# Sums of h for both parts of the down product on GpSimd, and one ring for all its operands

## The chip, the cores and the metric

The kernel runs on one core of a Trainium2 chip, in one launch. The metric is the device time of the launch in microseconds (us). Times are given as the median of several runs; beside them stands one profiled execution with its trace.

## The reference

The reference is one inference step of a trunk of two layers. Layer 0 mixes along the sequence by retention, layer 1 by gated linear attention (GLA); after each mixer comes a feed-forward block with a short convolution. There are 1024 new rows of a prompt and 32 rows of a running stream, together T = 1056 rows; the model width is 1024, the inner width of the feed-forward block 2816. Everything is float32. The block that the change touches is this one:

```python
def conv_ffn(h, conv_state, w_up, conv_w, conv_b, w_down):
    u = h @ w_up                                     # 1024 -> 2 * 2816
    T = u.shape[1]
    ext = jnp.concatenate([conv_state.astype(u.dtype), u], axis=1)
    c = conv_b + ext[:, 0:T] * conv_w[0]
    for j in range(1, CONV_W):
        c = c + ext[:, j:j + T] * conv_w[j]
    gate, val = jnp.split(c, 2, axis=-1)
    return (jax.nn.silu(gate) * val) @ w_down, ext[:, T:]   # 2816 -> 1024
```

The trunk adds the block's result to its input. In what follows `h` is the product `silu(gate) * val`, and the last line's product with `w_down` is the down product.

## The kernel before, in words

**Tiles.** `h` is kept transposed, with its 2816 columns on 22 tiles of 128 partitions and the 1056 rows along each tile. The up product makes tile `f` of both halves (`gate`, `val`) in turn, f = 0 to 21, in `ffn_up`; the convolution of a tile (`conv`) follows a little later and stores the tile to `scr_h` in DRAM (L1563, L1564).

**Products.** Every float32 operand is split into a high and a low part, and a product of two operands is three matmuls (high × high L333, high × low L337, low × high L338). On top of that, blocks of two by two are multiplied by the scheme of Strassen and Winograd: seven products instead of eight, each of them (`seven`) 12 matmuls of 128x264. In return sums of the blocks are needed as operands: of the weights (`wg`, `ws`, `wt`, `wv`, made by VectorE from `rg` and `rv`; `wsh` and `wsl` are the high and the low part of `ws`), and of the activations.

**Down product.** The first 16 tiles of `h` go through this scheme in two parts of 8 tiles (p = 0, 1); the other 6 tiles are done by another routine. For each part there are four pairs q of output tiles and two token halves s; a unit is (p, q, s), and the order of units is p, then q, then s. For each part and token half seven operands are wanted, numbered 1, 2, 5, 6, 7, 4, 3: three of them plain blocks of `h`, four of them sums. An operand is split by ScalarE (cast, the high part) and VectorE (subtraction, the low part) into its place in `X[s]` (`XA`, `XB`). Part two's operands take the places of part one's, when the last unit of part one on that half is through.

**Part one's sums (before).** Four pairs of tiles, (0, 4) to (3, 7): both tiles of a pair are loaded (`load_h`, L1380) into a work space `v` in the large buffer `AR`, VectorE makes four sums in place (`sum_h`, L1386, 128x528 elements each) while the up product runs, at f = 9, 11, 13, 15, and the result is stored to `scr_s` in DRAM (`sums_out`, L1389). When the up product ends, `part_one` queues fourteen pieces of 528 KB, plain blocks from `scr_h` and sums from `scr_s`; they come through a ring of four slots in `AR` (`pull`, L1396), each split (L1411 cast, L1412 subtraction), and each split pulls the next piece.

**Part two's sums (before).** Two raw loads of 1.08 MB per token half (`staged`, L1418) bring the eight tiles, and VectorE makes the four sums (L1432, 128x1056) between the splits (L1427, L1428). For token half 0 the raw loads are issued at the start of unit (0, 1, 1), after all open splits are emptied; for half 1 at the end of unit (0, 3, 1).

**What sets the order.** Each engine runs its own instructions in a fixed order, and waits for semaphores. All DMAs here are issued by SP (SyncE), whose queue is in order too: an issue that waits holds up those behind it. In the code the order comes from lists of small closures (`todo`), of which `step` runs two after each product. A product index k = 7f + i counts products of the up product for token half 0; half 1 follows some products later. One period of f has 14 products. The vector engine's chain in a period is: the weights' sums (L310 to L316), the low parts (L306), the additions out of PSUM (L1532) and the convolution (L1558, L1559, L1562). GpSimd does only small copies and memsets there (L1545, L1547, L1555, L1556).

The functions that the change touches:

Of the kernel before, what the change touches and what calls it, by code (L numbers as in the profile page):

```python
# [9 lines left out]
F32 = mybir.dt.float32  # L10
# [6 lines left out]
P = 128  # L17
# [35 lines left out]
def trunk_kernel(ctx: ExitStack, tc: tile.TileContext, io):  # L53
# [1308 lines left out]

    class Pieces:


        def __init__(self, l, X, AR, sm, room, early):
            self.l, self.X, self.sm, self.room, self.early = l, X, sm, room, early
            self.stg = [AR[:, o:o + KT * TH].rearrange("p (k t) -> p k t", k=KT) for o in SX]
# [9 lines left out]
        def load_h(self, k, after):  # L1378
            for a in range(2):
                order(nc.sync.dma_start(self.v[:, a], scr_h[k + 4 * a].rearrange("p (q t) -> p q t", q=4)), after)  # L1380

        def sum_h(self, j):

            b11, b12, b21, b22 = [self.v[:, a, o::2] for a in range(2) for o in range(2)]
            d, a, b = [(b12, b12, b11), (b22, b22, b12), (b11, b22, b11), (b21, b22, b21)][j]
            V.tensor_tensor(d, a, b, op=ALU.subtract)  # L1386
# [12 lines left out]
        def part_one(self):  # L1399
            for s in range(2):  # L1400
                a, b = [slice(t, t + TH) for t in (CQ[2 * s][0], CQ[2 * s + 1][0])]
                lo, hi = scr_h[0:4], scr_h[4:8]
                sm_ = scr_s.rearrange("k p (a t) -> k p a t", a=2)
# [11 lines left out]

        def staged(self, p, s, j):
            c0 = CQ[2 * s + j][0]
            nc.sync.dma_start(self.stg[j], scr_h[KT * p:KT * p + KT, :, c0:c0 + TH].rearrange("k p t -> p k t"))  # L1418

        def operands(self, s):  # L1420
            X = self.X[s]
            lo, hi = slice(0, 4), slice(4, 8)
            b11, b21, b12, b22 = [x[:, k] for x in self.stg for k in (lo, hi)]

            def split(o, v):
                def run():
                    S.copy(X[o][:, 0], v)  # L1427
                    V.tensor_tensor(X[o][:, 1], v, X[o][:, 0].bitcast(F32), op=ALU.subtract)  # L1428
                return run

            def minus(d, a, b):
                return lambda: V.tensor_tensor(d, a, b, op=ALU.subtract)  # L1432

            self.todo += [split(1, b11), minus(b12, b12, b11), split(2, b21), split(5, b12), minus(b12, b22, b12),
                          split(6, b12), minus(b11, b12, b11), split(7, b11), minus(b21, b12, b21), split(4, b21),
                          split(3, b22)]
# [22 lines left out]
        def run(self):  # L1459
# [14 lines left out]
            def one(u, m):  # L1474
# [12 lines left out]
                if m == 3:  # L1487
# [3 lines left out]
                    if q == NPAIR - 1 and p == 0:  # L1491
                        while self.todo:
                            self.step()
                        if s:
                            for j in range(2):
                                self.staged(1, s, j)
                        self.operands(s)

            for n, u in enumerate(units):
                p, q, s = u  # L1500
                order_ = (1, 2, 5, 6, 7, 4) if q == 0 else (1, 2, 6, 5, 7, 4)
                for i, m in enumerate(order_):
# [4 lines left out]
                    if u == (0, 1, 1) and i == 0:  # L1507
                        while self.todo:
                            self.step()
                        for j in range(2):  # L1510
                            self.staged(1, 0, j)
# [3 lines left out]
                    self.step()  # L1515
# [3 lines left out]
    def ffn_up(l, X, todo, fc, sm, nxt, after):  # L1519
# [50 lines left out]
        for n, (_, s, k) in enumerate(sorted(seq)):  # L1570
# [3 lines left out]
            if f == NF - 1:  # L1574
                if s == 0 and i == 2:
                    nxt.part_one()
# [13 lines left out]
            if s == 1 and i % 2 == 0 and 8 <= f <= 16 and f % 2:  # L1590
                nxt.sum_h(i // 2)
            if s == 0 and i == 5 and 8 <= f <= 16:
                if f % 2 == 0:
                    if f > 8:
                        nxt.sums_out((f - 10) // 2)
                    if f < 16:
                        nxt.load_h((f - 8) // 2, stored[0])
# [240 lines left out]
def _layout(inp):  # L1838
# [10 lines left out]
    def cols(v):  # L1849
# [46 lines left out]
            "scr_w": (2, 2, NPAIR, 2, P, D), "scr_g": (16, P, T), "scr_s": (4, P, 2 * T), "scr_qk": (RH, 2, 2, P, T)}  # L1896
# [30 lines left out]
```

## Time and profile before

| | |
|---|---|
| median of 3 runs | 2854.89 us (2853.45 to 2854.96) |
| profiled execution | 2849.49 us, its span 2847.7 us |
| mean granted TensorE clock | 0.995 |
| busy: TensorE (PE) | 2784.6 us, 98% |
| busy: VectorE (DVE) | 2109.5 us, 74% |
| busy: ScalarE (ACT) | 1320.2 us, 46% |
| busy: GpSimd (POOL) | 278.5 us, 10% |

The profiled execution is one run of its own, and its time is a little under the three others. A row of the timeline gives the start in us from the span's start, the duration, the engine, the line in the kernel, the operation, and what it writes and reads; in brackets stands how long the engine had been idle and what ended that. A row of groups gives the count, the total busy time and the mean duration in ns. PE's busy time runs matmuls together that follow each other in the pipeline; where TensorE loses time is better read from the number of matmuls in a stretch.

In layer 0 the up product lies roughly at 915 to 1365 us of the span and the two parts of the down product follow until about 1545; in layer 1 the up product ends near 2585, and part two begins near 2680.

### The profile page before, as it was taken

Reading aid. Unit: us, or ns where it says so; the run is one execution under the profiler, and the core shown is the slowest. Engines: PE = TensorE matmul, PEld = TensorE weight load, DVE = VectorE, ACT = ScalarE, POOL = GpSimd, SP = SyncE. Lnnn points to the kernel's source line nnn. Section 1 sums busy time; section 2 is a strip of 40 time slices with the busy share of each in tenths; the row PEclk is TensorE's granted clock in tenths of the full one; section 3 lists DMA queues with packets and bytes.
Section 4 is the critical chain, followed back from the end, with each engine's and each line's share of the span. In section 5 each row is a group of like instructions: output and inputs, shape, how many; then the busy total and the mean of one; then the engine's idle time right before and its main releaser. Section 6 shows DMA issues by size and latency. Waiting matters only on the chain.

```text
span 2847.7 us, 52541 instructions
## 1 busy us (share of the span) xinstructions
PE 2784.6 (98%) x20954; PEld 2681.9 (94%) x20954; DVE 2109.5 (74%) x3506; ACT 1320.2 (46%) x2395; POOL 278.5 (10%) x516
## 2 busy tenths in 40 slices
PE   8999999999999999999999999999999999999998
PEld 7999977888999999999999899999999999999997
DVE  7777777777578877877775677774478878788756
ACT  8433344444455444445443555553245444445424
POOL 1000000000001111111000232220011111110001
PEclk9999999999999999999999999999999999999999
DMA  6333386664865223332866301114522233428673
GB/s 218 110 123 106 118 269 205 213 198 150 273 203 192 76 75 121 129 129 94 284 216 240 122 27 46 52 44 143 198 85 75 73 116 115 150 70 278 205 232 116
DMA packets 232326, 419.35 MB, mean 147 GB/s; under 512 B 27376, under 2 KB 145776, under 8 KB 231056
## 3 DMA queue, kind: packets, MB, share of 16 engines
q1 hardware_dynamic: 231536, 415.40, 43.6%
q8 instruction: 164, 2.69, 0.4%
q14 instruction: 82, 0.67, 0.1%
q10 hardware_dynamic: 544, 0.59, 0.1%
HBM read 292.08 MB, written 123.85 MB: 146 GB/s over the span
## 4 chain that ended last, share of the span: by engine, by line
PE 82%; DVE 7%; DMA 4%; ACT 4%; issue 1%; POOL 1%; SPq 0%; DVEq 0%; ACTq 0%; POOLq 0%
PE pu L338 16%; PE pu L333 16%; PE pu L337 16%; PE pd L1281 4%; PE pd L1280 4%; PE pd L1282 4%; PE psv L238 2%; PE psv L237 1%; PE psv L236 1%; PE pj L124 1%; PE pj L126 1%; PE pj L125 1%; PE pg L124 1%; PE pg L125 1%; PE pg L126 1%
## 5 line engine op out<-in xcount | busy, mean ns | idle before, releaser
L104 DVE TENSOR_TENSOR wlo<-raw,whi 128x1024 fp32r<-128x1024 f32 x146 | 180.7, 1241 | 100.9 <-ACT whi L104 44.9
L1536 ACT COPY AR<-pu 128x264 f32<-128x264 f32 x264 | 99.0, 375 | 295.2 <-PE pu L338 292.4
L338 PE MATMUL pu<-XA,wgl 128*128 128x264 f32 x752 | 213.6, 284 | 0.0
L333 PE MATMUL pu<-XA,wgh 128*128 128x264 f32 x752 | 213.0, 283 | 0.0
L337 PE MATMUL pu<-XA,wgh 128*128 128x264 f32 x752 | 213.0, 283 | 0.0
L104 ACT CAST whi<-raw 128x1024 fp32r<-128x1024 f32 x146 | 152.3, 1048 | 110.7 <-DMA raw<-w_ro 38.0
L1280 PE MATMUL pd<-XB,whi 128*128 128x264 f32 x552 | 157.9, 286 | 1.6 <-DVE rm L208 1.6
L1558 DVE SCALAR_TENSOR_TENSOR AR<-AR,cw 128x1058 f32<-128x1058 f32 x88 | 115.8, 1317 | 57.7 <-ACT AR L1557 57.4
L1282 PE MATMUL pd<-XB,wlo 128*128 128x264 f32 x552 | 157.0, 284 | 0.0
L1281 PE MATMUL pd<-XB,whi 128*128 128x264 f32 x552 | 156.7, 284 | 0.0
L333 PE MATMUL pu<-XA,wsh 128*128 128x264 f32 x520 | 148.6, 286 | 1.7 <-ACT AR L1536 0.9
L338 PE MATMUL pu<-XA,wsl 128*128 128x264 f32 x520 | 148.3, 285 | 0.8 <-DVE wsl L306 0.8
L337 PE MATMUL pu<-XA,wsh 128*128 128x264 f32 x520 | 147.7, 284 | 0.0
L1532 DVE TENSOR_TENSOR AR<-AR,pu 128x264 f32<-128x264 f32 (+2 forms) x440 | 144.6, 368 | 0.0
L306 DVE TENSOR_TENSOR wtl<-rv,wth 128x1024 fp32r<-128x1024 f32 x58 | 71.6, 1234 | 98.5 <-ACT wth L305 97.1
L333 PEld LDWEIGHTS pu<-XA,wgh 128*128 128x128 f32 x752 | 141.3, 188 | 0.0
L338 PEld LDWEIGHTS pu<-XA,wgl 128*128 128x128 f32 x752 | 141.2, 188 | 0.0
L337 PEld LDWEIGHTS pu<-XA,wgh 128*128 128x128 f32 x752 | 141.2, 188 | 0.0
L333 PE MATMUL pu<-XA,whi 128*128 128x264 f32 x448 | 127.5, 285 | 1.8 <-ACT XA L1427 1.2
L338 PE MATMUL pu<-XA,wlo 128*128 128x264 f32 x448 | 127.1, 285 | 1.6 <-DVE wlo L104 1.6
L337 PE MATMUL pu<-XA,whi 128*128 128x264 f32 x448 | 126.9, 284 | 0.5 <-DVE XA L1412 0.3
L333 PE MATMUL pu<-XA,wth 128*128 128x264 f32 x408 | 116.4, 285 | 0.7 <-ACT wth L305 0.7
(481 smaller groups left out, 10528.0 us busy)
## 6 DMA issues: line engine op xcount, KB each, us to landing
raw<-w_ro SPq DMA_DIRECT2D x52, 512.0 KB, 4.7
rg<-w_up SPq DMA_DIRECT2D x44, 512.0 KB, 3.6
rv<-w_up SPq DMA_DIRECT2D x44, 512.0 KB, 3.5
scr_h<-AR SPq DMA_DIRECT2D x44, 512.0 KB, 2.7
AR<-scr_x SPq DMA_DIRECT2D x32, 528.0 KB, 4.9
scr_x<-AR SPq DMA_DIRECT2D x32, 528.0 KB, 3.5
raw<-scr_w SPq DMA_DIRECT2D x32, 512.0 KB, 4.8
AR<-scr_h SPq DMA_DIRECT2D x28, 528.0 KB, 4.8
```

The source lines that it names most:

```text
L104: ins = S.copy(hi, raw), V.tensor_tensor(lo, raw, hi.bitcast(F32), op=ALU.subtract)
L124: PE.matmul(ps, hi[:, k], rh, start=kt == 0, stop=False)
L306: V.tensor_tensor(l_, src, h.bitcast(F32), op=ALU.subtract)
L333: mm = PE.matmul(ps, wh[:, k], x[:, 0, kt], start=m in (1, 2, 4, 5) and kt == 0, stop=False, skip_group_check=True)
L337: PE.matmul(ps, wh[:, k], x[:, 1, kt], start=False, stop=False, skip_group_check=True)
L338: mm = PE.matmul(ps, wl[:, k], x[:, 0, kt], start=False, stop=kt == 3, skip_group_check=True)
L1280: PE.matmul(o, w[0][:, k], h[0][:, :n], start=i == 0, stop=False)
L1281: PE.matmul(o, w[0][:, k], h[1][:, :n], start=False, stop=False)
L1282: self.last_mm = PE.matmul(o, w[1][:, k], h[0][:, :n], start=False, stop=i == nk - 1)
L1532: V.tensor_tensor(u[:, d:d + n], t[:, o:o + n], b[:, o:o + n], op=op)
L1536: S.copy(t, b)
L1558: V.scalar_tensor_tensor(cj, uj[:, 1:T + 3], cw[:, nt, 1:2], cj, op0=ALU.mult, op1=ALU.add)
```

## The change

All sums for both parts are now made ahead, by GpSimd. `sum_h` issues its subtraction on GpSimd in place of VectorE (line 1388 of the changed kernel). There are eight pairs of tiles instead of four, (0, 4) to (3, 7) and (8, 12) to (11, 15). A table `SUMS` says at which product k a pair is loaded; its four sums are called 5, 7, 9 and 11 products later, its store 12 later. `scr_s` in DRAM has eight entries instead of four.

`operands` queues 28 pieces instead of 14, both parts and both halves, and the pieces of part two come through the same ring of four slots (line 1398 of the changed kernel). The raw loads `staged`, the subtractions on VectorE for part two and the emptying of the list at unit (0, 1, 1) are gone. Between products one split is run instead of two, but for the units of q = 0 in part one.

```diff
+    SUMS = (42, 56, 70, 84, 97, 109, 121, 133)
...
-            self.stg = [AR[:, o:o + KT * TH].rearrange("p (k t) -> p k t", k=KT) for o in SX]
...
         def load_h(self, k, after):
             for a in range(2):
-                order(nc.sync.dma_start(self.v[:, a], scr_h[k + 4 * a].rearrange("p (q t) -> p q t", q=4)), after)
+                order(nc.sync.dma_start(self.v[:, a], scr_h[k + k // 4 * 4 + 4 * a].rearrange("p (q t) -> p q t", q=4)),
+                      after)
...
-            V.tensor_tensor(d, a, b, op=ALU.subtract)
+            G.tensor_tensor(d, a, b, op=ALU.subtract)
...
-        def part_one(self):
-            for s in range(2):
+        def operands(self):
+            for p, s in ((0, 0), (0, 1), (1, 0), (1, 1)):
                 a, b = [slice(t, t + TH) for t in (CQ[2 * s][0], CQ[2 * s + 1][0])]
-                lo, hi = scr_h[0:4], scr_h[4:8]
-                sm_ = scr_s.rearrange("k p (a t) -> k p a t", a=2)
+                lo, hi = scr_h[KT * p:KT * p + 4], scr_h[KT * p + 4:KT * p + 8]
+                sm_ = scr_s[4 * p:4 * p + 4].rearrange("k p (a t) -> k p a t", a=2)
...
-        def staged(self, p, s, j):
-            c0 = CQ[2 * s + j][0]
-            nc.sync.dma_start(self.stg[j], scr_h[KT * p:KT * p + KT, :, c0:c0 + TH].rearrange("k p t -> p k t"))
-
-        def operands(self, s):
...
-            self.todo += [split(1, b11), minus(b12, b12, b11), split(2, b21), split(5, b12), minus(b12, b22, b12),
-                          split(6, b12), minus(b11, b12, b11), split(7, b11), minus(b21, b12, b21), split(4, b21),
-                          split(3, b22)]
...
                         while self.todo:
                             self.step()
-                        if s:
-                            for j in range(2):
-                                self.staged(1, s, j)
-                        self.operands(s)
+                        self.splits()
...
-                    if u == (0, 1, 1) and i == 0:
-                        while self.todo:
-                            self.step()
-                        for j in range(2):
-                            self.staged(1, 0, j)
...
-                    self.step()
+                    self.step(1 if p or q else 2)
...
-                    nxt.part_one()
+                    nxt.operands()
...
-            if s == 1 and i % 2 == 0 and 8 <= f <= 16 and f % 2:
-                nxt.sum_h(i // 2)
-            if s == 0 and i == 5 and 8 <= f <= 16:
-                if f % 2 == 0:
-                    if f > 8:
-                        nxt.sums_out((f - 10) // 2)
-                    if f < 16:
-                        nxt.load_h((f - 8) // 2, stored[0])
+            for j, at in enumerate(SUMS if s == 0 else ()):
+                if k == at + 12:
+                    nxt.sums_out(j)
+                if k == at:
+                    nxt.load_h(j, stored[0])
+                if k - at in (5, 7, 9, 11):
+                    nxt.sum_h((k - at - 5) // 2)
...
-            "scr_w": (2, 2, NPAIR, 2, P, D), "scr_g": (16, P, T), "scr_s": (4, P, 2 * T), "scr_qk": (RH, 2, 2, P, T)}
+            "scr_w": (2, 2, NPAIR, 2, P, D), "scr_g": (16, P, T), "scr_s": (8, P, 2 * T), "scr_qk": (RH, 2, 2, P, T)}
```

GpSimd's order in the up product of layer 0. Before (the copies of the edges `cst` at L1555, L1556, the setting up of the next u buffer at L1545, L1547):

```order
L1547 COPY AR_7512<-cc_7507 128x2
L1545 MEMSET AR_7512 128x2x2
L1547 COPY AR_7512<-cc_7507 128x2
L1555 COPY cst_7508<-AR_7512 128x2
L1556 COPY cst_7508<-AR_7512 128x2
```

And of the changed kernel, where the same copies are lines 1527 and 1528 and the same setting up lines 1517 and 1519:

```order
L1517 MEMSET AR_7512 128x2x2
L1519 COPY AR_7512<-cc_7507 128x2
L1527 COPY cst_7508<-AR_7512 128x2
L1528 COPY cst_7508<-AR_7512 128x2
L1388 TENSOR_TENSOR AR_7512<-AR_7512 128x2x264 x4
L1527 COPY cst_7508<-AR_7512 128x2
L1528 COPY cst_7508<-AR_7512 128x2
```

The four sums of a pair stand directly one behind the other, between the edge copies of the two halves of one tile, although the code calls them two products apart.

SP's order in the same place of the changed kernel (1535 and 1536 store a tile of `h`, 1381 loads a pair, 299 and 300 load the weights `rg` and `rv`, 1391 stores the sums):

```order
L1535 DMA scr_h<-AR_7512 128x1024
L1536 DMA scr_h<-AR_7512 128x32
L1381 DMA AR_7512<-scr_h 128x1056 x2
L299 DMA rg_11500<-w_up 128x1024
L1391 DMA scr_s<-AR_7512 128x2112
L300 DMA rv_11501<-w_up 128x1024
```

The store of the sums, which waits for GpSimd, stands between the pair of weight loads of one f.

SP's order at the border from part one to part two, layer 0. Before (`scr_x` is the running result, loaded at L1480 and stored at L1489; 102 and 1444 load weights):

```order
L102 DMA raw_15949<-w_dn 128x1024
L1489 DMA scr_x<-AR_7512 256x1x528
L1480 DMA AR_7512<-scr_x 128x2x528
L102 DMA raw_15955<-scr_w 128x1024
L102 DMA raw_15961<-scr_w 128x1024
L1418 DMA AR_7512<-scr_h 128x8x264
L1489 DMA scr_x<-AR_7512 256x1x528
L1418 DMA AR_7512<-scr_h 128x8x264
L1444 DMA rv_15968<-w_dn 128x512
L1480 DMA AR_7512<-scr_x 128x2x528
```

And of the changed kernel (there 1460 and 1469 load and store the running result, 1424 loads weights):

```order
L1398 DMA AR_7512<-scr_s 128x4x264 x2
L102 DMA raw_15980<-w_dn 128x1024
L1469 DMA scr_x<-AR_7512 256x1x528
L102 DMA raw_15986<-scr_w 128x1024
L102 DMA raw_15992<-scr_w 128x1024
L1424 DMA rv_15999<-w_dn 128x512
L1398 DMA AR_7512<-scr_s 128x4x264
L1398 DMA AR_7512<-scr_h 128x4x264
```

The two raw loads are replaced by pieces, and the last two pieces of part two stand behind four weight loads.

More of the change, by code (lines that the diff above doesn't have):

```diff
@@ L1414, in splits @@
             self.todo += [run] * 7
-        def staged(self, p, s, j):
-            c0 = CQ[2 * s + j][0]
-            nc.sync.dma_start(self.stg[j], scr_h[KT * p:KT * p + KT, :, c0:c0 + TH].rearrange("k p t -> p k t"))
-        def operands(self, s):
[L1421 to L1432, printed above, removed]
-            self.todo += [split(1, b11), minus(b12, b12, b11), split(2, b21), split(5, b12), minus(b12, b22, b12),
-                          split(6, b12), minus(b11, b12, b11), split(7, b11), minus(b21, b12, b21), split(4, b21),
-                          split(3, b22)]
         def weights(self, p, q):
```

## The prediction

> **What bounds the kernel now.** I read the page's busy times first, then the windows of the two feed-forward layers, then the instructions around each place where TensorE loses time, and last the VectorE chain of the up product.
>
> ```profile
> PE 2784.6 (98%) x20954; PEld 2681.9 (94%) x20954; DVE 2109.5 (74%) x3506; ACT 1320.2 (46%) x2395; POOL 278.5 (10%) x516
> ```
>
> TensorE is busy for 98% of the span, and the change adds and removes no matmul. Its matmuls are modelled as pipelined, so the loss has to be read from their pace. These windows show it (columns: busy us and count of PE, PEld, DVE, ACT, POOL; granted clock; DMA share; GB/s):
>
> ```profile
> core 0: us, PE busy (x) PEld busy (x) DVE busy (x) ACT busy (x) POOL busy (x), PEclk, DMA share, GB/s
> 940.00:1340.00 400.00, 400.00 (x3299) 400.00 (x3298) 320.82 (x471) 183.12 (x258) 55.53 (x139) 1.00 0.30 104
> 1340.00:1395.00 55.00, 52.17 (x416) 50.69 (x415) 48.81 (x60) 34.78 (x44) 3.37 (x8) 1.00 0.84 274
> 1450.00:1490.00 40.00, 37.64 (x286) 36.45 (x285) 30.45 (x37) 16.26 (x23) 0.00 (x0) 0.96 0.65 217
> 2560.00:2620.00 60.00, 57.63 (x460) 56.17 (x459) 52.38 (x65) 36.66 (x47) 3.60 (x10) 1.00 0.78 256
> 2675.00:2715.00 40.00, 37.29 (x296) 36.18 (x295) 31.52 (x37) 16.97 (x25) 0.00 (x0) 1.00 0.68 226
> ```
>
> In the up product of layer 0 (940 to 1340) TensorE never waits: 400.00 / 3299 = 0.12125 us per matmul, which is the pace of this kernel. Against it, 1450 to 1490 loses 40.00 − 286 × 0.12125 = 5.3 us, and 2675 to 2715 loses 40.00 − 296 × 0.12125 = 4.1 us. These two are the borders from part one to part two of the down product, 9.4 us together. The granted clock is 0.96 in the first of them; the windows without a wait have 1.00, so I count that to the wait, and if it has a cause of its own, 0.04 × 40 = 1.6 us of the 5.3 stay. The other two, 55.00 − 416 × 0.12125 = 4.6 and 60.00 − 460 × 0.12125 = 4.2 us, are the way from the up product into the down product; there the ring of four slots runs already, and the change leaves its first pieces as they are.
>
> What is late at the border of layer 0 (start, duration, engine, line; the bracket is idle time and what ended it):
>
> ```profile
> 1458.00 0.28 PE L338 MATMUL pu<-XA,wv 128*128 128x264 f32 x1
> 1459.29 0.39 PE L333 MATMUL pu<-XA,whi 128*128 128x264 f32 x1 [1.02 <-ACT XA L1427]
> 1460.27 0.39 PE L333 MATMUL pu<-XB,whi 128*128 128x264 f32 x1 [0.59 <-ACT XB L1427]
> 1467.05 0.39 PE L333 MATMUL pu<-XB,whi 128*128 128x264 f32 x1 [0.55 <-ACT XB L1427]
> 1458.17 1.07 ACT L1427 CAST XA<-AR 128x1056 fp32r<-128x1056 f32 x1 [2.64 <-DMA AR<-scr_h]
> 1450.17 0.38 SPq L1418 DMA_DIRECT2D AR<-scr_h  x1
> 1454.95 0.56 SPq L1489 DMA_DIRECT2D scr_x<-AR  x1
> 1455.56 0.72 SPq L1418 DMA_DIRECT2D AR<-scr_h  x1
> ```
>
> The chain runs from the raw loads of token half 1 (L1418): the second is issued only at 1455.56, behind a store of results (L1489). ScalarE waits 2.64 us for the first, TensorE waits for ScalarE's cast, and the subtractions (L1432) stand between the later casts. Only four loads per layer do this, but TensorE needs all seven operands of the half within one unit.
>
> **The change, part by part.** *Part two's raw loads and subtractions go.* These are the costs that leave (DVE rows: count | busy us, mean ns):
>
> ```profile
> L1432 DVE TENSOR_TENSOR AR<-AR 128x1056 f32<-128x1056 f32 x16 | 20.0, 1253 | 4.6 <-DMA AR<-scr_h 4.6
> L1386 DVE TENSOR_TENSOR AR<-AR 128x528 f32<-128x528 f32 x32 | 22.5, 705 | 6.2 <-DMA AR<-scr_h 6.1
> L1428 DVE TENSOR_TENSOR XA<-AR,XA 128x1056 fp32r<-128x1056 f32 x16 | 19.9, 1253 | 11.9 <-ACT XA L1427 7.9 <-PE pu L338 3.8
> DMA to landing us min/median/max: 6.3/7.3/8.1
> DMA to landing us min/median/max: 3.9/5.0/6.2
> DMA to landing us min/median/max: 3.9/4.7/5.7
> ```
>
> VectorE is rid of 20.0 us in the down product and 22.5 us in the up product. Neither is time by itself: VectorE is off the path except at the borders. What counts is that the wait is gone with its cause: 5.3 + 4.1 = **−9.4 us**, if the new feed keeps up. The three last rows are the landing times of the raw loads (L1418), of the ring's pieces (L1396) and of the pair loads (L1380); a piece lands in 5.0 us where a raw load took 7.3.
>
> *Part two's operands come by the ring.* One slot's cycle is load, cast and subtraction: 5.0 + 1.07 + 1.25 = 7.3 us, so four slots give one piece per 1.83 us. A product takes 12 × 0.12125 = 1.455 us and uses one piece, so the ring is slower than TensorE and lives on its lead: the units of part one's last pairs need no new pieces. I walked the fourteen pieces of part two through SP's and VectorE's new order, with landing times as above. Pieces 8 to 12 (token half 1) are ready between 1446.9 and 1456.7, before TensorE wants the first at 1458.1. The 13th and 14th pull stand on SP behind four weight loads of the next pair; they are ready at 1465.7 and 1466.9, wanted at 1458.1 + 5 × 1.455 = 1465.4 and some four products later. So the thirteenth is about 0.3 us late, by a walk that is itself good to about a microsecond. Bounds: nothing from below, from above what the same ring loses at its first use, 4.6 + 4.2 = 8.8 us. I take 1.0 us per layer, **+2.0 us**, near the lower end: at its first use the ring starts with two pieces and an empty lead, here with four and a lead of two units.
>
> *All 32 sums per layer go to GpSimd, in the up product.* In the new order the four sums of a pair stand directly behind each other, so GpSimd works in 8 bursts per layer, 16 in all, every second f. The trace has no such instruction of 128x528 elements; nearest are (POOL rows):
>
> ```profile
> L943 POOL TENSOR_TENSOR d<-b 128x384 f32<-128x384 f32 x56 | 51.0, 918 | 137.5 <-DVE x L951 57.1 <-DVE b L925 40.6 <-DVE gss L1133 39.5
> L149 POOL TENSOR_TENSOR ss<-ss,sq 128x264 f32<-128x264 f32 x24 | 22.6, 941 | 294.8 <-ACT sq L138 292.9 <-DVE XB L1254 1.9
> ```
>
> GpSimd has room (55.53 of 400 us). The question is what VectorE loses meanwhile. At the program's start both do the same kind of sum at once:
>
> ```profile
> 13.03 5.06 POOL L149 TENSOR_TENSOR NB<-NB 128x384 f32<-128x384 f32 x3 [12.59 <-ACT NB L138]
> 13.42 1.84 DVE L149 TENSOR_TENSOR NB<-NB 128x384 f32<-128x384 f32 x2
> 15.18 2.03 DVE L104 TENSOR_TENSOR wlo<-raw,whi 128x1024 fp32r<-128x1024 f32 x1
> 17.14 1.36 DVE L149 TENSOR_TENSOR NB<-NB 128x384 f32<-128x384 f32 x1
> 30.28 0.55 DVE L149 TENSOR_TENSOR NB<-NB 128x384 f32<-128x384 f32 x1
> 9.10 1.23 DVE L104 TENSOR_TENSOR wlo<-raw,whi 128x1024 fp32r<-128x1024 f32 x1 [1.12 <-ACT whi L104]
> ```
>
> Alone VectorE's four would take 3 × 0.55 + 1.23 = 2.88 us; beside GpSimd they take 13.42 to 18.50, 5.08 us. So three GpSimd sums cost VectorE 2.2 us, 0.73 each, or 0.73 × 528/384 = 1.0 each of the new ones: 4.0 us per burst. GpSimd's own burst is then 4 × 5.06/3 × 528/384 = 9.3 us. Bounds for VectorE's loss: 0 if the two do not meet, and the dearest row, 941 ns for 264 elements, taken whole: 4 × 2 × 0.94 = 7.5 us.
>
> The Trainium skill, page "SBUF — State Buffer", in its section on the two separate sides of the memory, says that VectorE and GpSimd share a pair of ports under an exclusive lock held for a whole instruction, which a VectorE instruction with two operands in SBUF takes part in. The trace agrees in kind (2.03 against 1.23 us); by that rule alone every GpSimd sum would stand in VectorE's way in full, which is the upper bound's case and the second rival below.
>
> Who waits for VectorE is the weights. Its chain in one period of the up product:
>
> ```profile
> 1170.64 1.22 DVE L306 TENSOR_TENSOR wsl<-rg,wsh 128x1024 fp32r<-128x1024 f32 x1
> 1171.89 0.33 SPq L300 DMA_DIRECT2D rv<-w_up  x1
> 1175.55 0.69 DVE L310 TENSOR_TENSOR rv<-rv 128x512 f32<-128x512 f32 x1
> 1178.81 1.23 DVE L306 TENSOR_TENSOR wtl<-rv,wth 128x1024 fp32r<-128x1024 f32 x1 [2.57 <-ACT wth L305]
> 1183.67 0.29 PE L338 MATMUL pu<-XA,wtl 128*128 128x264 f32 x1
> 1176.44 1.22 SPq L1380 DMA_DIRECT2D AR<-scr_h  x2
> ```
>
> A period is fourteen products of 1.455 us, 20.4 us. `wsl` frees the buffer for the next load, that load feeds L310, and `wtl` stands behind L310. A delay of `wsl` is taken up by the 2.57 us in which VectorE waits for ScalarE and by the 1183.67 − 1180.04 = 3.63 us until TensorE uses `wtl`: 6.2 us of cover. A burst begins when the pair has landed (1176.44 + 4.7, plus the issue of two), some nine microseconds ahead of the next `wsl`, so its 4.0 us reach `wsl` nearly whole. 4.0 < 6.2: **0 us**. Without cover left it would be 7.5 − 6.2 = 1.3 us per burst, 16 × 1.3 = 21 us. Between bursts lie two periods, in which VectorE has 20% idle (320.82 of 400), some 8 us: the delay is worked off.
>
> *Added waits.* The store of the sums (L1391 of the change) waits on SP for GpSimd, and behind it stands the next weight load `rv`. That load waits for `wsl` anyway, and the burst (1182 to 1191) ends ahead of the delayed `wsl` of the next period (1170.64 + 20.4 + 1.2 + 4.0 = 1196): nothing, and a burst that lasted 5 us longer would make the store the later one. Behind the burst on GpSimd stand the small copies and memsets of the two u buffers, wanted a period later: nothing. Part two's stored sums add 4 × 1.08 MB per layer against removed raw loads, in windows where the DMA queues are 0.30 busy: nothing.
>
> **Sum:** −9.4 + 2.0 + 0 = −7.4 us. Against the profiled execution, 2849.5 us (span 2847.7 and 1.8 around it), that gives 2842.1. The median of the runs is 2854.9, 5.4 above, so I forecast **2847.5 us** on the median. Between 2845.5 (no ring loss) and 2849 lies the forecast's own range.
>
> **Rivals.** *The ring is as slow as at its first use.* For it: the cycle of 1.83 us against 1.455, and the pulls that stand behind weight loads. Against it: four slots are filled early. Then 8.8 of the 9.4 us come back, −0.6: 2854 us, no change.
>
> *GpSimd keeps VectorE out for longer than the cover.* One mechanism at one place: `wtl` comes late in every f with a burst. For it, with VectorE only 20% idle, stands a two-column copy on GpSimd that took 1.22 us while VectorE was at work, and 0.19 us after:
>
> ```profile
> 1167.83 1.31 DVE L1559 SCALAR_TENSOR_TENSOR AR<-AR,cw 128x1058 f32<-128x1058 f32 x1
> 1167.98 1.22 POOL L1556 COPY cst<-AR 128x2 f32<-128x2 f32 x1
> 1169.28 0.19 POOL L1547 COPY AR<-cc 128x2 f32<-128x2 f32 x1
> ```
>
> So they exclude each other at least in part. Against it: 0.73 us per sum of 384 measured, and VectorE's additions out of PSUM need not meet it. It decides from 6.2 us per burst; at 7.5 us the time is 2847.5 + 21 = 2868 us, slower.
>
> *The sums come too late.* The last pair is loaded at k = 133 of 154 and its sums are stored by 145, while the ring first wants a sum of part two after the whole of part one; I give this nothing of its own.
>
> **Chances.** Forecast 0.58, ring as slow as before 0.24, GpSimd in the way 0.18. A measurement of this kernel tells about 0.2% (5.7 us) from no change; the forecast lies 7.4 below, so its chance is that of faster, 0.58; same 0.24, slower 0.18. The range runs from 2843.5 (the whole 9.4 and 2 more for VectorE's relief) to 2859, which holds the first rival and the mild end of the second, where the cover is passed by a quarter of a microsecond per burst.
>
> **What would show it.** Right: the borders' windows at 0.12125 us per matmul with at most 1 us lost each, no wait for XB above a few tenths; L1388 on GpSimd at 1.3 to 2.3 us each; TensorE without a wait in 940 to 1340, `wtl` done ahead of its matmul though L306 and L1530 show stretched instances. Wrong: waits of `pu<-XA,wtl` or of `wsl` on VectorE in every second f (the second rival); waits on ring pieces behind weight loads at the borders (the first); or a border's loss that stays although the operands are early, which would mean that the weights or the results were late there too.

## The result and the profile after

The changed kernel takes 2870.01 us (median of 5 runs, 2864.05 to 2876.39); the kernel before, timed beside it, 2853.45 us (5 runs, 2852.31 to 2854.96). The ratio is 1.0057, with a 95% interval of 1.0038 to 1.0077: some 16 us **slower**, where 2847.5 us and faster was forecast and 2859 was the upper end of the range. The profiled execution took 2864.05 us, span 2862.2 us, 14.5 us more than before.

The busy times of the changed kernel, and the same stretches of its span as shown of before (busy us and count of PE, PEld, DVE, ACT, POOL; granted clock; DMA share; GB/s):

```profile
PE 2783.5 (97%) x20954; PEld 2678.2 (94%) x20954; DVE 2121.3 (74%) x3458; ACT 1318.6 (46%) x2395; POOL 398.2 (14%) x580
940.00:1340.00 400.00, 394.28 (x3219) 392.46 (x3218) 327.70 (x446) 178.58 (x252) 108.22 (x167) 1.00 0.36 124
1450.00:1490.00 40.00, 39.08 (x317) 38.41 (x316) 30.16 (x37) 20.57 (x29) 0.00 (x0) 1.00 0.90 308
2165.00:2560.00 395.00, 387.80 (x3174) 385.70 (x3174) 326.01 (x441) 177.15 (x250) 109.05 (x165) 1.00 0.35 123
2675.00:2715.00 40.00, 37.89 (x307) 37.25 (x307) 32.80 (x39) 21.89 (x31) 0.00 (x0) 1.00 0.94 312
```

At 0.12125 us per matmul the up product of layer 0, which lost nothing before, now loses 400.00 − 3219 × 0.12125 = 9.7 us, that of layer 1 395.00 − 3174 × 0.12125 = 10.2. VectorE is busy for 7 us more in layer 0's (327.70 against 320.82), although it makes 16 sums fewer. The border of layer 0 loses 1.6 us where it lost 5.3.

The kernels do not reach the same work at the same time, so a second reading is used from here on: the start of the n-th matmul in one trace minus the start of the n-th in the other, over the same n. It gives what a stretch costs (us; stretches named by the times of the kernel before, minus is a gain):

| kernel | up product, layer 0 (940 to 1340) | border, layer 0 (1395 to 1490) | up product, layer 1 (2165 to 2560) | border, layer 1 (2600 to 2715) |
|---|---|---|---|---|
| changed kernel | +9.4 | −3.7 | +7.9 | 0.0 |

Which wait it is shows in the groups of TensorE. First the row of before, then that of the changed kernel (the first of three matmuls with the weights `wsh`; count, busy us, mean ns, idle before and what ended it):

```profile
L333 PE MATMUL pu<-XA,wsh 128*128 128x264 f32 x520 | 148.6, 286 | 1.7 <-ACT AR L1536 0.9 <-DVE AR L1532 0.7
```

```profile
L333 PE MATMUL pu<-XA,wsh 128*128 128x264 f32 x520 | 150.1, 289 | 14.7 <-DVE AR L1504 12.6 <-ACT AR L1508 1.6
```

Not the weights are late, but L1504, VectorE's addition out of PSUM. Of the eight bursts per layer seven end in such a wait, of 0.15 to 1.84 us, always at product m = 3 of token half 0. The longest in layer 0, with VectorE's work ahead of it, GpSimd's burst, and TensorE's wait (changed kernel):

```profile
1271.87 1.22 DVE L306 TENSOR_TENSOR wgl<-rg,wgh 128x1024 fp32r<-128x1024 f32 x1
1273.01 1.81 DVE L315 TENSOR_TENSOR wv<-rv,wv 128x512 fp32r<-128x512 f32 x1
1274.75 1.81 DVE L311 TENSOR_TENSOR rg<-rv,rg 128x512 f32<-128x512 f32 x1
1276.48 0.38 DVE L1504 TENSOR_TENSOR AR<-AR,pu 128x232 f32<-128x232 f32 x1
1276.79 1.51 DVE L312 TENSOR_TENSOR rg<-rg 128x512 f32<-128x512 f32 x1
1278.22 1.82 DVE L316 TENSOR_TENSOR rv<-rv,rg 128x512 f32<-128x512 f32 x1
1280.06 1.31 DVE L1531 SCALAR_TENSOR_TENSOR AR<-AR,cw 128x1058 f32<-128x1058 f32 x1
1281.29 0.42 DVE L1504 TENSOR_TENSOR AR<-AR,pu 128x264 f32<-128x264 f32 x1
1272.52 6.97 POOL L1388 TENSOR_TENSOR AR<-AR 128x528 f32<-128x528 f32 x4 [3.92 <-DMA AR<-scr_h]
1281.76 0.39 PE L333 MATMUL pu<-XA,wsh 128*128 128x264 f32 x1 [1.84 <-DVE AR L1504]
```

The same place in the kernel before, a few periods earlier:

```profile
1184.27 1.22 DVE L306 TENSOR_TENSOR wgl<-rg,wgh 128x1024 fp32r<-128x1024 f32 x1
1185.41 0.68 DVE L315 TENSOR_TENSOR wv<-rv,wv 128x512 fp32r<-128x512 f32 x1
1186.01 0.68 DVE L311 TENSOR_TENSOR rg<-rv,rg 128x512 f32<-128x512 f32 x1
1186.62 0.39 DVE L1532 TENSOR_TENSOR AR<-AR,pu 128x232 f32<-128x232 f32 x1
1186.92 0.68 DVE L312 TENSOR_TENSOR rg<-rg 128x512 f32<-128x512 f32 x1
1187.52 0.68 DVE L316 TENSOR_TENSOR rv<-rv,rg 128x512 f32<-128x512 f32 x1
1189.46 0.42 DVE L1532 TENSOR_TENSOR AR<-AR,pu 128x264 f32<-128x264 f32 x1
1192.16 0.28 PE L333 MATMUL pu<-XA,wsh 128*128 128x264 f32 x1
```

Before, `wgl` starts at 1184.27 and the addition ends at 1189.88: 5.61 us; then 2.28 us pass until TensorE starts m = 3. In the changed kernel the same way takes 1271.87 to 1281.71, 9.84 us: 4.23 us more. 4.23 − 2.28 = 1.95 us, and TensorE starts m = 3 2.0 us late. The code says why m = 3 waits there: it adds into the PSUM bank `c` which m = 5 filled, and the addition for m = 7 must have read that bank before. So this is a wait inside the scheme of seven products; by the code another PSUM bank would not lift it, which no run tried.

The stretching itself is one for one. Four VectorE instructions with both operands in SBUF (`wv`, L311, L312, L316, each 0.68 us before, as their rows show) are 1.13, 1.13, 0.83 and 1.14 us longer, one for each sum; the addition with an operand in PSUM that lies among them is not (0.38 us, 0.39 before). More such additions fall beside sums in a later run, the kernel with the burst behind m = 3: there 58 of them (128x264) take 0.42 us in the median, like the 191 others in the two up products. The Trainium skill, page "SBUF — State Buffer", section "Who interferes with whom", says that VectorE with two SBUF inputs and a GpSimd instruction that reads SBUF block each other for a whole instruction, and that VectorE with at most one SBUF input does not take part unless it runs in a mode that uses two ports; these rows agree with both halves of it.

### The profile page after: what moved, and what is told of

The parts are those of the page before. It is cut to its first block, busy times and chain, and to the rows that moved or that the text cites. A ratio compares the mean times of both kernels' runs of the same rounds, so it can differ in the third digit from the quotient of the medians.

```text
span 2862.2 us, 52654 instructions
## 1 busy us (share of the span) xinstructions
PE 2783.5 (97%) x20954; PEld 2678.2 (94%) x20954; DVE 2121.3 (74%) x3458; ACT 1318.6 (46%) x2395; POOL 398.2 (14%) x580
## 2 busy tenths in 40 slices
DMA packets 242247, 443.15 MB, mean 155 GB/s; under 512 B 28080, under 2 KB 152624, under 8 KB 239952
## 4 chain that ended last, share of the span: by engine, by line
PE 73%; DVE 13%; DMA 5%; ACT 4%; issue 3%; POOL 1%; SPq 0%; DVEq 0%; ACTq 0%; POOLq 0%
PE pu L333 14%; PE pu L338 14%; PE pu L337 13%; PE pd L1281 3%; PE pd L1280 3%; PE pd L1282 3%; PE psv L238 2%; PE psv L237 2%; PE psv L236 2%; DVE wgl L306 1%; PE pj L124 1%; PE pj L126 1%; PE pj L125 1%; PE pg L124 1%; PE pg L125 1%
## 5 line engine op out<-in xcount | busy, mean ns | idle before, releaser
L1504 DVE TENSOR_TENSOR AR<-AR,pu 128x264 f32<-128x264 f32 (+2 forms) x440 | 144.1, 366 | 0.0
L149 POOL TENSOR_TENSOR ss<-ss,sq 128x264 f32<-128x264 f32 (+2 forms) x39 | 38.9, 997 | 745.7 <-ACT sq L138 743.8
L1529 ACT ACTIVATE AR<-AR,cw 128x1058 f32<-128x1058 f32 x88 | 111.9, 1271 | 55.8 <-DVE AR L1504 52.6
L333 PE MATMUL pu<-XA,whi 128*128 128x264 f32 x448 | 127.3, 284 | 2.0 <-ACT AR L1451 1.9
```

The lines of the kernel that those rows point to most:

```text
L333: mm = PE.matmul(ps, wh[:, k], x[:, 0, kt], start=m in (1, 2, 4, 5) and kt == 0, stop=False, skip_group_check=True)
L1504: V.tensor_tensor(u[:, d:d + n], t[:, o:o + n], b[:, o:o + n], op=op)
L1529: S.activation(cj, uj[:, 2:T + 4], AF.Identity, scale=cw[:, nt, 2:3], bias=cw[:, nt, 3:4])
```

## The experiments

**One chip, four kernels: who makes the sums, how many, how they are spaced, and where.** The theory is that VectorE's 4.2 us are passed on to TensorE where an addition has only 2.3 us of cover. The rivals are the doubled pair loads and stores, GpSimd's own queue, and a cost for every sum without a threshold. The kernel before had 2849.64 us there; chips differ by a few us, so each ratio is against the kernel before on the same chip.

All sums on VectorE:

```diff
-            G.tensor_tensor(d, a, b, op=ALU.subtract)
+            V.tensor_tensor(d, a, b, op=ALU.subtract)
```

> The changed kernel with one edit: the 32 sums per layer are made by VectorE instead of GpSimd; pairs, stores and the ring are as in the change. Theory: four GpSimd sums in a row lengthen VectorE's instructions beside them by about 4.2 us, one addition out of PSUM behind them then frees its PSUM bank too late (it has 2.3 us of cover), and TensorE waits in 7 of 8 bursts per layer; that is the 9.7 and 10.2 us lost in the two up products. On VectorE a sum takes 0.7 us and the four do not stand together in its order, so TensorE should not wait in 940 to 1340 and 2165 to 2560: about 20 us less than the changed kernel, 2846 to 2851 us. Rival one, the doubled pair loads and stores on SP and the DMA queues: nothing changes, 2865 to 2870. Rival two, GpSimd's edge copies and memsets stand behind the sums and the u buffers come late: also 2846 to 2851, so this run does not part it from the theory.

Measured 2849.33 us, ratio 0.9994 (0.9985 to 1.0003). The up product at pace:

```profile
940.00:1340.00 400.00, 400.00 (x3297) 399.85 (x3296) 332.09 (x490) 183.72 (x257) 58.52 (x140) 1.00 0.36 125
```

The doubled loads and stores are all there (DMA share 0.36, as in the changed kernel) and cost the up product nothing. That rival falls. VectorE is busier than in the changed kernel (332.09 against 327.70 us) and still in time.

Two of four sums:

```diff
-                if k - at in (5, 7, 9, 11):
+                if k - at in (5, 7):
```

> The changed kernel with two of the four sums of each pair left out (the other two are stored unsummed, so the result of the down product is not the reference's). A burst is half as long. Theory (a cover of 2.3 us, then a wait): half a burst costs VectorE about 2.1 us, so hardly any wait of TensorE for an addition is left, 0 to 0.3 us per burst; 2846 to 2852 us. Rival, every GpSimd sum costs TensorE its share, without a threshold: half of the 20 us stays, about 2860 us. Rival, transfers: 2865 to 2870.

Measured 2848.31 us, ratio 0.9993 (0.9984 to 1.0002). Half a burst costs the up products nothing at all, not half. So where these bursts fall there is a threshold, and it lies between two and four sums in a row.

Each sum paced by the product beside which it is called:

```diff
-            G.tensor_tensor(d, a, b, op=ALU.subtract)
+            tc.add_manual_dep(G.tensor_tensor(d, a, b, op=ALU.subtract).ins, mm.ins.name,
+                              mybir.DependencyInfo(mybir.DependencyClass.Sync, mybir.DependencyReason.DATA),
+                              reason="pace")
```

> The changed kernel with one edit: each sum on GpSimd also waits for the last matmul of the product beside which it is called, so the four of a pair start some 5.8 us apart (two products of each token half) instead of one behind the other. Theory: each sum costs VectorE about 1 us, less than the 2.3 us of cover, and VectorE has a fifth of its time to make it up before the next: no wait of TensorE in the up products; 2846 to 2851 us, below the kernel before. Rival, GpSimd's own queue (edge copies and memsets behind the sums): the queue is now blocked for over 20 us per pair instead of 7, so it gets worse than 2870. Rival, transfers: nothing changes, 2865 to 2870.

Measured 2853.74 us, ratio 1.0011 (1.0001 to 1.0020): the 16 us are gone, as the theory had it, but the time was above the 2846 to 2851 expected, though the profiled execution (2849.27 us) loses nothing between 940 and 1340 and between 2165 and 2560 us. A second series of the same kernel, at the end of the study, asked whether pacing has a cost of its own.

> The kernel whose GpSimd sums are each paced by a product, once more: its runs had a median 4 us over the kernel before although its profiled execution showed no wait in the up products. If that was one chip's spread, it now stands within 2 us of the kernel before; if pacing has a cost of its own (GpSimd's edge copies and memsets behind a waiting sum), it stands 3 to 6 us above it again, and the profile of this execution should show TensorE waiting in the up products or at the borders.

It gave 2851.52 us against 2850.67, ratio 1.0002 (0.9992 to 1.0011). By the medians most of the 4 us were spread between series. The traces show a cost all the same, just behind the stretches above: by the n-th matmul both paced executions lose 2.5 and 2.2 us between 1340 and 1395 and 1.5 and 1.2 us between 2560 and 2600, where the kernel with the burst behind m = 3 loses nothing. There the first two pieces of the ring stand on SP behind the store of the last sums; in the first paced execution they are issued at 1333.64, against 1328.11 with the burst behind m = 3, and TensorE waits twice for the addition (0.22 and 0.70 us). That the late ring is the reason is likely, but not shown. Within the up products the rival falls: GpSimd's queue, in which the four sums of a pair now stretch over 19 us, costs nothing there.

Part one's sums alone on GpSimd, in the kernel before:

```diff
             d, a, b = [(b12, b12, b11), (b22, b22, b12), (b11, b22, b11), (b21, b22, b21)][j]
-            V.tensor_tensor(d, a, b, op=ALU.subtract)
+            G.tensor_tensor(d, a, b, op=ALU.subtract)
```

> The kernel before with one edit: part one's 16 sums per layer are made by GpSimd; part two is as before, with raw loads and VectorE's subtractions, and there are no more loads or stores than before. Theory: four bursts per layer, each a wait of about 1.2 us with what follows, some 8 to 10 us more than the kernel before, 2861 to 2864 us; the borders to part two lose their 5.3 and 4.1 us as before. Rival, transfers: the time of the kernel before, 2853 us.

Measured 2856.7 us, ratio 1.0023 (1.0013 to 1.0033): slower by 6.6 us, without a single added transfer. Two of its four bursts per layer end in a wait for the addition, of 0.64 to 0.93 us, and a third in layer 0 in one of 0.12 us. 8 to 10 us were expected: the sign and the place are the theory's, the size is not, since not every burst meets the addition. That asked for the next runs.

**Same burst, other place.** If the place in VectorE's period decides, then four sums in a row must be free at one place and dear at another. On one chip (the kernel before 2849.78 us) ran the changed kernel once more, and two in which the burst waits for a chosen product of token half 0:

> The changed kernel as it is, once more, so that it stands on one chip beside the next three. Theory and rivals alike: 12 to 20 us over the kernel before, with waits of TensorE at product m = 3 (pu<-XA,wsh) in 7 of 8 bursts per layer.

2868.48 us, ratio 1.0064 (1.0050 to 1.0078), with waits at m = 3 behind all eight bursts of layer 0 and six of layer 1.

Burst behind product m = 3 (i = 6), that is, just behind the addition:

```diff
-                if k - at in (5, 7, 9, 11):
-                    nxt.sum_h((k - at - 5) // 2)
+                if 5 <= k - at < 12 and k % 7 == 6:
+                    for x in range(4):
+                        nxt.sum_h(x, mm)
```

> The changed kernel with the same four sums in a row on GpSimd, but each burst waits for the last matmul of a product m = 3 of token half 0, the point just behind the addition that TensorE waited for. Theory (it is the place of the burst in VectorE's period that decides, not its length): the next 4.2 us that VectorE loses fall where it has 2.6 and 1.9 us of idle time, and the next addition with little cover is a period away; no wait of TensorE for an addition, 2846 to 2851 us where the kernel before has 2849.6. Rival, the number of GpSimd sums or their length sets the loss: 12 to 20 us over the kernel before, as the change.

2850.02 us, ratio 1.0000 (0.9991 to 1.0009). And behind the third product (`k % 7 == 2`), so that the burst lies on the way to the addition:

> As the run before it, but each burst waits for the last matmul of the third product of token half 0 (i = 2), so that all four sums fall on the busy stretch of VectorE that ends in the addition which product m = 3 waits for. Theory: the addition comes 4 x 1.13 = 4.5 us later, of which 2.3 us are covered: a wait of about 2 us in every burst, 16 x 2 = 32 us and up to 1.6 us more for each burst where the granted clock falls to half after the wait; 2880 to 2905 us. Rival, number or length of the sums: 12 to 20 us over the kernel before, as the change.

2880.0 us (two runs), ratio 1.0103 (1.0084 to 1.0121), 30 us slower. The up product of layer 0 in the two kernels, first with the burst behind m = 3, then ahead of the addition, and one of the waits of the latter:

```profile
940.00:1340.00 400.00, 400.00 (x3298) 400.00 (x3297) 325.39 (x454) 183.59 (x258) 111.31 (x170) 1.00 0.37 127
```

```profile
940.00:1340.00 400.00, 389.72 (x3183) 388.08 (x3182) 326.60 (x441) 176.89 (x250) 103.21 (x163) 1.00 0.33 118
1200.32 0.39 PE L333 MATMUL pu<-XA,wsh 128*128 128x264 f32 x1 [1.37 <-DVE AR L1506]
```

The same 32 sums per layer on GpSimd, with GpSimd busy for 111 and 103 us (the last burst of the second kernel lies behind the stretch), cost nothing or 30 us. The rival of number and length falls; the place decides. The dear one was expected at 2 us per burst and shows 1.4 in most, because the first sum falls in part where VectorE is idle and lengthens only the instruction ahead, by 0.4 us: VectorE reaches the addition 3.8 us late there, and 3.8 − 2.28 = 1.5, what TensorE loses.

**The border.** With the up products repaired, the first part of the forecast should have come out: 7 us below the kernel before. It did not; 0.9994 and 1.0000 are 2 us at most. The differences by the n-th matmul (us):

| kernel | up, layer 0 | border, layer 0 | up, layer 1 | border, layer 1 |
|---|---|---|---|---|
| sums on VectorE | 0.0 | −3.6 | 0.0 | −1.4 |
| two of four sums | 0.0 | −1.8 | 0.0 | −1.9 |
| paced | 0.0 | −3.1 | 0.0 | −0.4 |
| part one alone (border as before) | +3.0 | −1.5 | +2.4 | −0.2 |
| changed kernel again | +9.9 | −2.6 | +7.9 | −1.3 |
| burst behind m = 3 | 0.0 | −3.0 | 0.0 | +0.7 |
| burst ahead of the addition | +15.4 | −3.3 | +12.0 | +2.6 |

The kernel whose border was not touched shows −1.5: the profiled execution of before held a stretch of half clock at that border that not every execution has. So the ring itself gains between 0.3 and 2.1 us of 5.3 in layer 0, and in layer 1, the last row left aside, between −0.7 and 1.9 us of 4.1. What stands in the place of the raw loads' wait is seen with the sums on VectorE:

```profile
1446.23 1.07 ACT L1413 CAST XA<-AR 128x1056 fp32r<-128x1056 f32 x1 [2.15 <-DMA AR<-scr_h]
1447.21 0.37 ACT L1451 COPY AR<-pu 128x264 f32<-128x264 f32 x1
1447.63 0.39 PE L333 MATMUL pu<-XB,whi 128*128 128x264 f32 x1 [1.06 <-ACT AR L1451]
```

No operand is late for TensorE at this border. ScalarE stands for 2.15 us in a cast that waits for its piece, and behind the cast stands the copy of a finished product out of PSUM, for which TensorE waits 1.06 us (1.58 in layer 1). First a little room in ScalarE's order was tried, on the same chip as the shifted bursts:

```diff
-                    self.step(1 if p or q else 2)
+                    if (u, i) != ((1, 0, 0), 1):
+                        self.step(1 if p or q else 2)
```

> All sums on VectorE, as in the earlier run of that kind, and one split less early: between the second and the third product of unit (1, 0, 0) no split is issued, so the sixth and later pieces of part two are cast one product later in ScalarE's order. Theory on the border: ScalarE stood in a cast that waited up to 2.9 us for its piece, and the copy out of PSUM (L1451) behind it held TensorE for 1.06 us in layer 0 and 1.58 us in layer 1; one product (1.455 us) of room takes most of this away, so the border's wait for L1451 near 1447 and 2672 falls to 0 to 0.5 us each; 1 to 3 us less in all than with the sums on VectorE alone, 2845 to 2849 us where the kernel before has 2849.6. Rival: the ring as a whole is too slow (1.83 us a piece against 1.455 a product), then the wait only moves to a later piece and the time is as with the sums on VectorE alone.

2848.89 us, ratio 0.9995 (0.9987 to 1.0004); the waits for the copy were 1.30 and 1.06 us in layer 0 and 1.80 in layer 1. No gain: the wait moved along, as the rival had it. Then the pieces themselves were made smaller, in the kernel with the burst behind m = 3 (`n4` is 2 in part two and 4 in part one):

```diff
-                nc.sync.dma_start(v, src)
+                nc.sync.dma_start(v[:, :n4], src[:, :n4])
```

> The kernel with the bursts behind m = 3, and of each piece of part two only the first half is loaded (two of its four tiles; the other half of the operand is what lay in the slot, so the down product is not the reference's). Theory on the border: the casts of part two wait on ScalarE for pieces that land late because the DMA queues are 90% busy there (before 65%), and the copies out of PSUM (L1453 there) behind these casts hold TensorE; with half the bytes the pieces land in 3 to 4 us, the casts wait for none, and the border's loss goes from about 2.3 us (layer 0) and 4.8 us (layer 1) to under 1 us each: 2843 to 2847 us where the kernel before has 2849.7. Rival: the pulls are late on SP, behind stores and weight loads, whatever they carry: the waits and the time stay, 2849 to 2851.

2846.28 us against 2849.76, ratio 0.9982 (0.9973 to 0.9991), where whole pieces had 1.0000: some 5 us less, and the borders gain 3.9 and 3.4 us by the n-th matmul. The landing times of the ten pieces of part two that are issued at the border, first whole (burst behind m = 3; layer 0, 1425 to 1490, then layer 1, 2655 to 2715), then halved (the same stretches):

```profile
DMA to landing us min/median/max: 3.9/6.3/7.7
DMA to landing us min/median/max: 3.8/6.6/8.8
```

```profile
DMA to landing us min/median/max: 2.7/4.5/6.0
DMA to landing us min/median/max: 2.7/4.6/5.5
```

So the size of the pieces, and not the place of the pulls on SP alone, holds the border for the larger part. The two are not parted altogether: with half pieces the slots come free sooner, and the last two pulls of layer 0 come 19 us behind the first of the border instead of 28. What is left, waits of 0.3 to 0.8 us for the same copy, may be SP's. A half piece has half the rows as well as half the bytes; the next run asks which of them counts.

In the same kernel, with whole pieces, the sums were then laid out in DRAM so that a piece is read in longer rows (the reading side follows):

```diff
-            nc.sync.dma_start(scr_s[k].rearrange("p (a q t) -> p a q t", a=2, q=4), self.v)
+            p, i = divmod(k, 4)
+            d = scr_s[8 * p:8 * p + 8, :, i * TH:(i + 1) * TH].rearrange("n p t -> p n t")
+            nc.sync.dma_start(d, self.v.rearrange("p a q t -> p (a q) t"))
```

> The kernel with the bursts behind m = 3, and the stored sums laid out in DRAM by piece, so that a piece of sums is read as 4224 bytes in a row per partition instead of four rows of 1056 bytes (the stores write rows of 1056 instead; the result is the reference's). If the number of rows sets how long a piece takes: the eight pieces of sums per part land in about 4 us instead of 5 to 6, the casts wait less, and the border gains 1 to 3 us: 2846 to 2849 us, perhaps below the kernel before. If the bytes alone set it: no change, 2850 us.

2849.54 us, ratio 0.9994 (0.9984 to 1.0004): longer rows do not help by an amount that can be told, which leaves the bytes. Last, the two edits that each stood a little below the kernel before were put together:

> The two edits that each stood a little below the kernel before, together: all sums on VectorE, and the stored sums laid out by piece (4224 bytes in a row). Theory: no wait in the up products, the borders gain 3 to 5 us of their 9.4 as with the sums on VectorE alone; 2847 to 2849 us where the kernel before has 2849.7, at the edge of what can be told. Rival, the gain at the border is given back in full by the late pieces: 2850 us or more.

2849.76 us against 2850.67, ratio 0.9995 (0.9985 to 1.0004). The best kernels of the study thus stand level with the kernel before; none of those that do the whole work beats it by more than can be told.

## Why the prediction was wrong

**The step that failed** is the one that says "Who waits for VectorE is the weights", and with it the 6.2 us of cover. The weights' chain was read rightly (in each up product of the changed kernel `wtl` held up one weight load of TensorE, for 0.2 us, as before), but it was not the chain with the least cover. The addition for m = 7, with 2.28 us, was; it stands in VectorE's order behind five instructions on the weights and the convolution, and the next product writes the bank it reads. The price before it was right: 4.0 us of VectorE per burst were forecast, 4.23 measured, 1.13 per sum against 1.0. With the right cover the sum of that part would have been 4.0 − 2.3 = 1.7 us for each burst that lies on that way, 16 × 1.7 = 27 us at most, in place of 0; measured were 9.4 + 7.9 = 17.3 us, since only some bursts lie on it in full.

**The rival that came true** is the second, with a chance of 0.18 and 2868 us: GpSimd keeps VectorE out for longer than the cover. Its mechanism and its sign were right and its price was close (2870.01 measured), but for the wrong reason: it took 7.5 us against 6.2, where it is 4.2 against 2.3, and it named `wtl` where it is the addition. That 2868 came so close is luck: it holds 21 us for the up products, where 17.3 were lost, and −7.4 us for the borders, where −3.7 came. The upper end of the range, 2859, was said to hold that rival up to a quarter of a microsecond per burst; from 2847.5 it is 11.5 / 16 = 0.7 us.

**The border's −9.4 us** were the right loss, read at the right place, with one part, the 1.6 us of the half clock, that comes and goes. The raw loads' waits are gone, as forecast.

**The ring's +2.0 us** is a mis-sized term: by the changed kernel's table the borders gained 3.7 and 0.0 us of 9.4, so what took the place of the old waits cost 5.7, inside the bounds of 0 and 8.8 but far from the value taken. Its landing time was too short: 5.0 us were taken, and at the borders of the changed kernel the pieces landed in 6.2 and 6.4 us (medians), so four slots gave a piece per 2.1 to 2.2 us and not per 1.83. The walk asked only when TensorE wants each operand. The thirteenth, which it put 0.3 us late, held TensorE for 0.88 us in layer 1 and not at all in layer 0. It did not ask what stands behind a cast that waits, which on ScalarE is the copy out of PSUM. And the added transfers were called free by the share of the up product (0.30), while the pieces move at the border: over the 60 us around it the share went from 0.60 to 0.83 in layer 0 and from 0.62 to 0.82 in layer 1. They were undercounted, too. Where 4 × 1.08 MB per layer were named, the profiles' pages have 419.35 MB before and 443.15 MB after, 11.9 MB more per layer.

**The added waits** (store of the sums on SP, copies behind the burst on GpSimd) were costed at nothing, and the sums on VectorE and the burst behind m = 3 show that for the up products: both have the doubled loads and stores, and no loss. Just behind the up products, where the ring's first loads stand on SP behind such a store, the paced kernel lost 3 to 4 us in all, and this wait may be the reason.

**In the order list** it was seen that the four sums stand one behind the other. What that means in time was not used: nothing on GpSimd waits for TensorE, so a burst starts when its pair has landed, at whatever point of VectorE's period that is.

## What to carry to other kernels

Work given to an engine that stands idle is not free where it holds up a busy one: count what the busy engine loses (here 1.13 us for each sum of 528 elements), then look for the least cover among all who wait for that engine, the ones inside an accumulation too, and place the work where the cover is large. The same burst was worth 0 or 30 us by its place alone, and one dependence on a chosen product put it there.

Where loads are made smaller and more numerous, ask what stands behind the instruction that waits for each of them, on the engine that waits, and add up the transfers of the stretch in which they move.

## What the runs showed of the hardware that was not expected

A wait can cost more than it lasts. After the 1.84 us wait at 1281.76 fifteen matmuls followed at 0.22 us instead of 0.121, 1.6 us more, while the granted clock was half (changed kernel; three stretches that hold this wait and what follows it, then two that hold the end of a wait of 1.69 us in layer 1 and what follows that; the granted clock is the third number from the end):

```profile
1279.62:1283.03 3.41, 1.57 (x13) 1.36 (x12) 3.41 (x6) 2.48 (x3) 1.86 (x3) 1.00 0.76 317
1283.03:1286.44 3.41, 3.41 (x18) 3.41 (x18) 3.29 (x5) 1.09 (x1) 0.23 (x2) 0.50 0.35 117
1286.44:1289.85 3.41, 3.41 (x30) 3.41 (x30) 1.96 (x2) 0.86 (x2) 0.00 (x0) 1.00 0.49 196
2511.83:2515.24 3.41, 1.89 (x15) 1.89 (x16) 3.41 (x4) 2.46 (x3) 1.35 (x2) 1.00 0.30 121
2515.24:2518.66 3.42, 3.42 (x30) 3.42 (x29) 3.28 (x6) 1.47 (x2) 0.23 (x2) 1.00 0.47 153
```

The half clock begins about 1.3 us after TensorE has started again and lasts 3.41 us. The wait of 1.69 us had no such sequel, so length alone does not decide. What does is seen in the trace's record of the granted clock: the first three stretches of half clock of the changed kernel begin at 71.30, 760.79 and 1283.03 us, which is 202 and 153 times 3.413 us apart, and in every run of this study such stretches stand a whole number of these steps apart. The wait of 1.84 us lies in one step, in which TensorE was busy for 1.57 of 3.41 us. The wait of 1.69 us, from 2511.66 to 2513.35, is cut by the border of a step at 2511.83, and TensorE was busy for 1.89 of 3.41 us there. Both cases fit a rule by which a wait is dear when it leaves TensorE too little work in one step, with a limit near half; two cases do not fix it. The Trainium skill, page "TensorE: Matmul & The Clock Gate", section "Part 1: The HAM clock gate (the "warmup" mystery)", says that the clock is either half or full, by how busy TensorE was in a window that runs on by itself; the two values, the steps of 3.413 us and the different sequel of the two waits agree with it.
